# Layer 1's output projection as seven products of blocks, with weight sums made in DRAM, gate rows in the last head, and new orders from attention on

## The chip, the cores and the metric

The kernel runs on one core of a Trainium2 chip. The metric is the device time of one launch in microseconds. A core has a matrix engine (PE) with its weight loads (PEld), three engines for elementwise work (DVE, ACT and POOL), an engine SP that here only issues transfers, and DMA queues that carry data between DRAM and on-chip memory. Each engine works through its own instructions in program order and waits on semaphores for the others.

## The reference, cut to what matters

Two layers run over 512 latent and 256 context tokens of width 1024. Layer 0 is a hyena mixer and attention; layer 1, where the change lies, is a bidirectional mLSTM of eight heads with value width 256:

```python
def finish(h_f, h_b, o, z):
    h = (h_f + h_b).transpose(0, 2, 1, 3).reshape(Bn, n, ML_WIDTH).astype(o.dtype) * jax.nn.sigmoid(o)
    h = rms_norm(h.reshape(Bn, n, ML_HEADS, ML_V), head_norm.reshape(ML_HEADS, ML_V)).reshape(Bn, n, ML_WIDTH)
    return (h * jax.nn.silu(z)) @ w_out
...
x_lat = x_lat + ga_l[:, None] * rms_norm(y_lat, g_post[layer])
```

The product with w_out is 512 tokens x 2048 x 1024. Only the latent tokens are needed behind the last layer. ga_l is a third of silu(c) @ w_mod + b_mod: the "gate rows" below are these 1024 numbers, spread over all partitions and multiplied with g_post.

## The kernel before

All matrix products of activations with weights are made in three parts: each operand is split into a high part in a reduced float format (hi) and a remainder (lo), and `mm3` issues hi·hi, hi·lo and lo·hi into one PSUM tile. The ACT makes the high part by a cast, DVE the low part by a subtraction (`split`). `load_w` brings a block of weights in two chunks of 512 KB into raw tiles `wr` (three buffers) and splits them into one of two weight slots, `wh0/wl0` or `wh1/wl1`; the tiles then hold 8 k-tiles x 256 columns, or 4 k-tiles x 512 once they are viewed by `wide`.

The program is written as regions (start, hy, att, out0, l1a, l1b, out1). In each, the calls are recorded, and `play` issues them in the order of a table of numbers, ORDERS; a second table, SLOTS, says which buffer each tile takes. So all recorded instructions have one line in the profile, L1000 (L998 after the change), and are told apart by their tiles. Within an engine this order is program order.

Region l1b is the heads of layer 1. Each head has the state products, then a normalisation (tiles `num`, `dn`, `hh`, `hj`, `hst`, `hrs`), transposes through the PE into `pm`, and a store of the turned head, `y`, to `y1` in DRAM, 256 rows of 512 tokens. Between the products of a head `fill` places projections of the next head; the last head has the out gate (`out_gate`) and the gate z (`gate_z`) there, both with weights of the slots.

The output projection reads `y1` back. Its first 1024 rows of weights (heads 0 to 3) go as four stages of 256 columns, `pj` tiles of 128 tokens x 256: 4 stages x 4 token blocks x 8 k-tiles x 3 = 384 matmuls of 256 columns. The first stage's 96 are `ready` in region l1b, half of them ahead of the last head's transposes and half behind. The other 1024 rows go as 2 column halves x 2 parts x 4 blocks x 4 k-tiles x 3 = 192 matmuls of 512 columns, with the token tiles `hTh/hTl` and `ych/ycl`. All of it accumulates in `yacc`, half of it by DVE additions from PSUM.

In out1 `out_stages` calls `row(u)` and `spread(u)` of `gate_rows` between stages: `row` takes 2 MB of w_mod straight into a weight slot (two transfers of 1 MB) and runs 16 narrow matmuls for each of the halves hi and lo (`mod_rows`), `spread` turns the row into a tile with one wide matmul and multiplies it with g_post on DVE (`gg`). The end is `weigh1` (times gg), the squares of the ACT into `ss2`, `rstd` with a small POOL instruction (`ers`), and `epi1`, which scales, adds the residual `xt` and stores.

Earlier in the program, in region hy, the kernel already makes sums of weights in DRAM (`o_sums`) with copies that SP issues and accumulating transfers that POOL issues.

Of the kernel before, what the change touches and what calls it, by code (L numbers as in the profile page):

```python
# [2777 lines left out]
```

## Time and profile before

| what | us |
|---|---|
| three runs | 1490.02, 1491.35, 2872.85 |
| median | 1491.35 |
| profiled execution | 1491.61 |
| its span | 1489.8 |
| heads of layer 1 (l1b), from the span's start | about 1045 to 1392 |
| output projection of layer 1 behind the last head's transposes | 1392 to 1482 |

The profile comes from one execution of 1491.61 us. Its span, 1489.8 us, is the time between the first and the last recorded instruction. The highest of the three runs lies far from the other two, which agree within 0.1%. Busy times add up what an engine's instructions took; PE matmuls are pipelined and their ends are modelled, so that the mean of a single one in the groups is longer than the pace at which they follow one another. The pace is read from the chain of waits, where a row gives start, duration, engine and tile, and xN the number of instructions in the piece.

### The profile page before, as it was taken

The page shows a single profiled execution, that of the slowest core. Times are in us where ns is not written, and L with a number is a line of the kernel's source. Part 1 is how long each engine was busy: PE and PEld are TensorE (multiplying, and loading weights), DVE is VectorE, ACT ScalarE, POOL GpSimd, SP SyncE. Part 2 cuts the span into 40 slices and gives each one's busy share as a digit, 9 for nine tenths or more (in the row PEclk, how much of TensorE's full clock was granted, in tenths as well). Part 3 has the DMA queues.
Part 4 walks back from the last instruction along what each step waited for, and adds up shares of the span by engine and source line. Part 5 has one row for each costly group of instructions (what it writes and reads, how often), then busy time and mean ns, then how long its engine had stood idle before and what let it go on. Part 6 is the DMA issues. An engine that isn't in the chain of part 4 may idle for free. (4 is left out here: it accounts for less than half of the span.)

```text
span 1489.8 us, 25927 instructions
## 1 busy us (share of the span) xinstructions
PE 1457.7 (98%) x10362; PEld 1339.3 (90%) x10362; DVE 1037.1 (70%) x1927; ACT 766.3 (51%) x1577; POOL 82.5 (6%) x125
## 2 busy tenths in 40 slices
PE   7999999999999999999999989999999999999997
PEld 5889999989998998989997789999999999999986
DVE  6687777887865666668325888666777777877455
ACT  6634343434435444446332567645766676666442
POOL 1100000001010000000000100000100000100000
PEclk9999999999999999999999999999999999999999
DMA  9755565457331121233462334675433322324463
GB/s 378 221 140 144 146 162 131 147 140 183 76 100 43 54 96 54 82 117 114 164 222 68 134 123 155 203 267 198 156 117 97 113 62 86 124 88 140 153 205 123
DMA packets 57353, 205.79 MB, mean 138 GB/s; under 512 B 7003, under 2 KB 8539, under 8 KB 54448
## 3 DMA queue, kind: packets, MB, share of 16 engines
q1 hardware_dynamic: 50968, 181.85, 35.9%
q0 software_dynamic: 5392, 21.11, 7.4%
q8 instruction: 81, 1.33, 0.4%
q10 hardware_dynamic: 872, 1.18, 0.3%
q14 instruction: 40, 0.33, 0.1%
HBM read 182.06 MB, written 51.41 MB: 157 GB/s over the span
## 5 line engine op out<-in xcount | busy, mean ns | idle before, releaser
L1000 PE MATMUL pj<-wh,hTh 128*128 128x256 f32 (+2 forms) x1200 | 340.6, 290 | 0.8 <-ACT qjunk L1000 0.4
L1000 PE MATMUL pj<-wl,hTh 128*128 128x256 f32 (+2 forms) x1200 | 337.4, 287 | 0.3 <-DVE wl L1000 0.3
L1000 PE MATMUL pj<-wh,hTl 128*128 128x256 f32 (+2 forms) x1200 | 336.7, 288 | 0.0
L1000 PE MATMUL pj<-hTh,wh 128*128 128x512 f32 (+1 forms) x832 | 286.8, 346 | 0.4 <-DVE vl L1000 0.3
L1000 PE MATMUL pj<-hTl,wh 128*128 128x512 f32 (+1 forms) x832 | 285.4, 344 | 0.4 <-DVE hTl L1000 0.4
L1000 PE MATMUL pj<-hTh,wl 128*128 128x512 f32 (+1 forms) x832 | 285.5, 345 | 0.0
L1000 PEld LDWEIGHTS pj<-wh,hTh 128*128 128x128 f32 x1200 | 224.3, 189 | 6.2 <-issue 2.7
L1000 PEld LDWEIGHTS pj<-wl,hTh 128*128 128x128 f32 x1200 | 225.0, 189 | 2.9 <-DVE wl L1000 0.5
L1000 PEld LDWEIGHTS pj<-wh,hTl 128*128 128x128 f32 x1200 | 223.9, 189 | 3.5 <-issue 1.5
L1000 DVE TENSOR_TENSOR wl<-wr,wh 128x1024 fp32r<-128x1024 f32 (+1 forms) x142 | 171.4, 1213 | 63.9 <-ACT wh L1000 63.9
L1000 ACT CAST wh<-wr 128x1024 fp32r<-128x1024 f32 (+1 forms) x142 | 146.7, 1043 | 83.4 <-PE pj L1000 55.8
L1000 PEld LDWEIGHTS pj<-hTh,wh 128*128 128x128 f32 x832 | 156.6, 189 | 18.5 <-DVE vl L1000 1.1
L1000 PEld LDWEIGHTS pj<-hTl,wh 128*128 128x128 f32 x832 | 156.8, 189 | 17.9 <-DVE hTl L1000 0.7
L1000 PEld LDWEIGHTS pj<-hTh,wl 128*128 128x128 f32 x832 | 156.4, 188 | 18.0 <-DVE wl L1000 0.3
L1000 DVE TENSOR_TENSOR PTl<-pj,PTh 128x384 fp32r<-128x384 f32 (+1 forms) x80 | 41.1, 526 | 18.8 <-ACT PTh L1000 18.4
L1000 ACT CAST PTh<-pj 128x384 fp32r<-128x384 f32 (+1 forms) x80 | 35.6, 459 | 30.5 <-PE pj L1000 29.8
L1000 DVE TENSOR_TENSOR wl<-ch,wh 128x1024 fp32r<-128x1024 f32 x28 | 34.2, 1221 | 24.5 <-ACT wh L1000 24.4
L1000 DVE TENSOR_REDUCE mx<-s 128x1 f32<-128x768 f32 (+1 forms) x48 | 37.2, 775 | 11.4 <-PE s L1000 11.2
L1000 PE MATMUL pm<-Rh,dfa 128*128 128x256 f32 (+1 forms) x192 | 45.0, 305 | 0.0
L1000 DVE TENSOR_TENSOR med<-big 128x512 f32<-128x512 f32 (+1 forms) x48 | 40.4, 864 | 5.0 <-ACT big L1000 4.8
L1000 PE MATMUL s<-dfa,qTh 128*128 128x256 f32 (+1 forms) x160 | 42.8, 338 | 0.7 <-ACT hdh L1000 0.6
L1000 DVE SCALAR_TENSOR_TENSOR C<-C,apb,pj 128x258 f32<-128x258 f32 x64 | 30.8, 481 | 16.5 <-PE pj L1000 11.8
(374 smaller groups left out, 3172.1 us busy)
## 6 DMA issues: line engine op xcount, KB each, us to landing
wr<-in_e_w_in SPq DMA_DIRECT2D x52, 512.0 KB, 5.3
wr<-in_o_w_in SPq DMA_DIRECT2D x50, 512.0 KB, 5.2
o_sums<-in_o_w_in POOLq DMA_DIRECT2D x28, 512.0 KB, 7.1
ch<-o_sums SPq DMA_DIRECT2D x21, 512.0 KB, 4.9
wh<-in_w_mod SPq DMA_DIRECT2D x10, 1024.0 KB, 7.3
wl<-in_w_mod SPq DMA_DIRECT2D x9, 1024.0 KB, 7.6
wr<-in_e_w_out SPq DMA_DIRECT2D x16, 512.0 KB, 4.5
wr<-in_o_w_out SPq DMA_DIRECT2D x16, 512.0 KB, 4.6
```

Of the source, the lines that this page charges most:

```text
L1000: x = fn(*a, **k)
```

## The change

The projection becomes a product of two-by-two blocks with seven products in place of eight (the form of Strassen and Winograd). The tokens are cut into two blocks of 256 and the 2048 rows into heads 0 to 3 and 4 to 7, the columns into halves of 512, so that `w11, w12` come from the first thousand rows and `w21, w22` from the second. Each product is 256 tokens x 1024 x 512, 48 matmuls of 512 columns:

| product | tokens | weights | goes into |
|---|---|---|---|
| p1 | A11 | w11 | c11 and, as a base, c21 and c12 |
| q7 | D1 | t3 | c21 |
| q6 | F6 | t2 | c21, c12 |
| q3 | F3 | w22 | c12 |
| q5 | F5 | t1 | c22, c12 |
| p2 | A12 | w21 | c11 |
| q4 | A22 | t4 | c21 |

- The weight sums t1 to t4 stand in a new DRAM tensor `w_sums`. `out_sums` makes them in eight steps of four transfers of 512 KB each, issued behind heads 0 to 5 and 6; steps without a sum are copies of SP, the others accumulating transfers of POOL. The layout of the first half of w_out changes with it.
- The token forms are differences of blocks of y. In l1b POOL subtracts in place for D1; in out1 `forms(h)` loads heads h and 4 + h and POOL makes F6 and F5 (in place) and F3 (tile `yf3`), twelve subtractions of 128x512. Each form is then split by ACT and DVE: 20 splits of 128x512 in out1, where 8 stood before.
- p1 and q7 are in l1b, p1 with its first half ahead of the last transposes and its second behind. out1 has the other five.
- In out1 ten blocks of weights are loaded (20 chunks of 512 KB); with the 8 of p1 and q7 it is 28 for the projection, where 16 were. The three raw buffers and two slots stay.
- The gate rows move into the last head: `row(0)` between out_gate and gate_z, `spread(0)`, `row(1)` and `spread(1)` behind gate_z, into a tile `gg1` of a new pool.
- The tables of att, out0, l1a, l1b and out1 are new, and most of SLOTS. Those of start and hy are the same. l1b has 3871 entries instead of 3784, out1 426 instead of 661.

By engine the program has 9188 rows on the PE instead of 9391 (rows with xN count once), 1849 on DVE instead of 1821, 1376 on ACT instead of 1365, 129 on POOL instead of 102 and 375 on SP instead of 353.

The PE at the last head's transposes, before. The `pj` tiles here are the ready products (weights `wh_2470`, `wl_2471`, tokens `hTh`, `hTl`), the `pm` the transposes of `hh`:

```order
L1000 MATMUL pj_12064<-wh_2470_12056,hTl 128x256
L1000 MATMUL pj_12064<-wh_2470_12056,hTh 128x256
L1000 MATMUL pj_12066<-wh_2470_12056,hTh 128x256
L1000 MATMUL pj_12066<-wl_2471_12057,hTh 128x256
L1000 MATMUL pm_12055<-c_ident,hh_12041 128x128 x4
L1000 MATMUL pm_12054<-c_ident,hh_12041 128x128 x4
L1000 MATMUL pj_12067<-wh_2470_12056,hTh 128x256
L1000 MATMUL pj_12067<-wl_2471_12057,hTh 128x256
L1000 MATMUL pj_12067<-wh_2470_12056,hTl 128x256
```
The same place after. `pj_12078` and `pj_12079` are p1's two tiles, `pm_12052` the second gate row, `wh_2461` its weights, which lie in the slot that `wh_2485` takes next:

```order
L998 MATMUL pj_12079<-wl_2482_12071,hTh 128x512
L998 MATMUL pj_12079<-wh_2481_12070,hTl 128x512
L998 MATMUL pm_12069<-c_ident,hh_12055 128x128
L998 MATMUL pm_12068<-c_ident,hh_12055 128x128
L998 MATMUL pm_12052<-wh_2461_12050,cond_67 32x256 x5
L998 MATMUL pm_12069<-c_ident,hh_12055 128x128
L998 MATMUL pm_12068<-c_ident,hh_12055 128x128
L998 MATMUL pm_12069<-c_ident,hh_12055 128x128 x2
L998 MATMUL pm_12068<-c_ident,hh_12055 128x128
L998 MATMUL pm_12052<-wh_2461_12050,cond_67 32x256
L998 MATMUL pm_12068<-c_ident,hh_12055 128x128
L998 MATMUL pm_12052<-wh_2461_12050,cond_67 32x256 x2
```
Behind these come eight more of the row with `wl_2462`, and then p1 with the new slot:

```order
L998 MATMUL pm_12052<-wl_2462_12051,cond_67 32x256 x8
L998 MATMUL pj_12079<-wh_2485_12074,hTh 128x512
L998 MATMUL pj_12078<-wh_2485_12074,hTh 128x512
L998 MATMUL pj_12078<-wl_2486_12075,hTh 128x512
L998 MATMUL pj_12078<-wh_2485_12074,hTl 128x512
```
Before, the products around the transposes read one slot; now the row stands among the transposes, and the products behind it read the row's slot, newly filled.

DVE towards the end of out1, before: one weight split to a few additions and weightings of `yacc`.

```order
L1000 TENSOR_TENSOR yacc_2482_15884<-pj_15943,yacc_2482_15884 128x512
L1000 TENSOR_TENSOR yacc_2482_15884<-yacc_2482_15884,gg_15885 128x512
L1000 TENSOR_TENSOR yacc_2482_15884<-pj_15949,yacc_2482_15884 128x512
L1000 TENSOR_TENSOR yacc_2482_15884<-yacc_2482_15884,gg_15885 128x512
L1000 TENSOR_TENSOR yacc_2482_15884<-pj_15951,yacc_2482_15884 128x512
L1000 TENSOR_TENSOR wl_2552_15954<-wr_15955,wh_2551_15953 128x1024
L1000 TENSOR_TENSOR yacc_2482_15884<-yacc_2482_15884,gg_15885 128x512
L1000 TENSOR_TENSOR wl_2552_15954<-wr_15956,wh_2551_15953 128x1024
```
DVE towards the end of out1, after (`wl_2571` and `wl_2575` are q4's weights, `gg` the gate, `xt` the residual):

```order
L998 TENSOR_TENSOR wl_2571_16069<-wr_16071,wh_2570_16068 128x1024
L998 TENSOR_REDUCE ess_16079<-ss_2501_15999 128x1
L998 TENSOR_SCALAR esst_16080<-ess_16079 128x1
L998 TENSOR_TENSOR yacc_2502_16000<-yacc_2502_16000,gg_1586_11172 128x512
L998 TENSOR_REDUCE ess_16083<-ss_2501_15999 128x1
L998 TENSOR_SCALAR esst_16084<-ess_16083 128x1
L998 TENSOR_TENSOR yacc_2502_16000<-yacc_2502_16000,gg_1586_11172 128x512
L998 SCALAR_TENSOR_TENSOR xt_2578_16076<-yacc_2502_16000,ers_16081,xt_2578_16076 128x512
L998 TENSOR_TENSOR wl_2575_16073<-wr_16074,wh_2574_16072 128x1024
L998 SCALAR_TENSOR_TENSOR xt_2578_16076<-yacc_2503_16001,ers_16081,xt_2578_16076 128x512
L998 SCALAR_TENSOR_TENSOR xt_2578_16076<-yacc_2502_16000,ers_16085,xt_2578_16076 128x512
L998 TENSOR_TENSOR wl_2575_16073<-wr_16075,wh_2574_16072 128x1024
```
The epilogue of the first two token blocks now stands among the last weight splits.

POOL behind the last head's `hrs`, before: nothing but the four `ers`.

```order
L1000 TENSOR_TENSOR hrs_12052<-hst_12051,mhalf 128x4
L1000 TENSOR_TENSOR ers_15962<-esst_15961,mhalf 128x1
L1000 TENSOR_TENSOR ers_15967<-esst_15966,mhalf 128x1
L1000 TENSOR_TENSOR ers_15973<-esst_15972,mhalf 128x1
L1000 TENSOR_TENSOR ers_15979<-esst_15978,mhalf 128x1
```
After (`yraa` and `yrab` are the loaded heads h and 4 + h):

```order
L998 TENSOR_TENSOR yraa_16012<-yraa_16012,yrab_16013 128x2x256
L998 TENSOR_TENSOR yraa_16012<-yraa_16012 128x2x256
L998 TENSOR_TENSOR yf_2537_16035<-yrab_16013,yraa_16012 128x512
L998 TENSOR_TENSOR yraa_16014<-yraa_16014,yrab_16015 128x2x256
L998 TENSOR_TENSOR yraa_16014<-yraa_16014 128x2x256
L998 TENSOR_TENSOR yraa_16020<-yraa_16020,yrab_16021 128x2x256
L998 TENSOR_TENSOR yraa_16020<-yraa_16020 128x2x256
L998 TENSOR_TENSOR yf_2539_16037<-yrab_16021,yraa_16020 128x512
L998 TENSOR_TENSOR yf_2538_16036<-yrab_16015,yraa_16014 128x512
```
The subtractions of all four pairs stand there in a row, ahead of the `ers`; the two raw tiles of a pair rotate through two buffers each.

The diff, with its tables cut to a line:

```diff
@@ layout @@
-    o["o_w_out"] = slices(wo[:1024])
+    o["o_w_out"] = quarters(wo[:1024])
@@ ORDERS, SLOTS @@
     "att": [
...
@@ ahead of l1b @@
+    w11, w12 = (ins["o_w_out"][:, hf] for hf in range(2))
+    w21, w22 = (ins["o_w_out2"][:, hf] for hf in range(2))
+    wsum = nc.dram_tensor("w_sums", [4, 2, P, 8, 256], F32).ap()
+
+    def out_sums(step):
+        t = wsum
+        dst, src, add = ((t[0], w12, 0), (t[2], w12, 0), (t[0], w11, 1), (t[2], w22, 1),
+                         (t[1], t[0], 0), (t[1], w22, 1), (t[3], t[1], 0), (t[3], w21, 1))[step]
+        for q in range(2):
+            for k in range(2):
+                sl = slice(4 * k, 4 * k + 4)
+                if add:
+                    G.dma_start(dst[q, :, sl], src[q, :, sl], accum_op=ALU.add)
+                else:
+                    SP.dma_start(dst[q, :, sl], src[q, :, sl])
+
+    gg1 = T(es.enter_context(tc.tile_pool(name="gate", bufs=1, side="left", reuse_waits="tile")), "gg1", (P, 1, D))
@@ heads, last head @@
-            work = [(out_gate, i) for i in range(4)] + [(gate_z, i) for i in range(4)]
+            row, spread = gate_rows(gg1, gg1[:, 0], 1, 1)
+            work = [(out_gate, i) for i in range(4)] + [(row, 0)] + [(gate_z, i) for i in range(4)] + [(spread, 0), (row, 1), (spread, 1)]
@@ behind each head @@
+        for step in {6: (6, 7), 7: ()}.get(h, (h,)):
+            out_sums(step)
@@ end of l1b @@
+    def form(tiles, a):
+        return lambda k, j: tuple(x[:, k, a + j * P:a + (j + 1) * P] for x in tiles)
+
+    def part(ps, w, i, lhs, q):
+        for kt in range(4):
+            ins_ = mm3(ps, lhs(4 * q + kt, i), (w[0][:, kt], w[1][:, kt]), q == 0 and kt == 0, q == 1 and kt == 3)
+        return ins_
...
+        split(*[x[:, k:k + n, NL:NT] for x in hT_], raw[:, :, :256])
+        G.tensor_tensor(raw[:, :, 256:], raw[:, :, 256:], raw[:, :, :256], ALU.subtract)
...
+    ws = [wide(load_w(w11[q])) for q in range(2)]
+    p1 = [PJ() for _ in range(2)]
...
+    ws = [wide(load_w(wsum[2, q])) for q in range(2)]
+    q7 = [PJ() for _ in range(2)]
...
@@ out1 @@
+    def forms(h):
+        ra, rb = (T(op, f"yra{x}", (P, 2, NL), bufs=2) for x in "ab")
+        SP.dma_start(ra, y1[h])
+        SP.dma_start(rb, y1[4 + h])
+        kk = slice(2 * h, 2 * h + 2)
+        lo, hi = (slice(n * 256, (n + 1) * 256) for n in range(2))
+        G.tensor_tensor(ra[:, :, hi], ra[:, :, hi], rb[:, :, hi], ALU.subtract)
+        G.tensor_tensor(ra[:, :, lo], ra[:, :, lo], ra[:, :, hi], ALU.subtract)
+        split(*[x[:, kk] for x in f6], ra[:, :, lo])
...
+    w = load(t2, 0)
...
+    q6 = pair()
+    both(q6, F6, w, 0)
...
+    q4 = pair()
+    for j in range(2):
+        for q, x in enumerate((w, wn)):
+            part(q4[j], x, j, A22, q)
+        V.tensor_tensor(c21[:, j], q4[j], c21[:, j], ALU.subtract)
+        weigh(0, 2 + j)
+        epilogue(2 + j)
```

More of the change, by code (lines that the diff above doesn't have):

```diff
@@ L754 @@
     "pm@3": [
[4 rows of a table removed]
[4 rows of a table added]
     ],
     "g@4": [
-        0, 1, 0, 1, 0, 1, 0, 1,
+        1, 0, 1, 0, 1, 0, 1, 0,
     ],
     "x0s@4": [
-        0, 1, 0, 1, 0, 1, 0, 1,
+        1, 0, 1, 0, 1, 0, 1, 0,
     ],
@@ L853 @@
     "xn@9": [
-        1, 0, 1, 2, 2, 0, 1, 2, 0, 1, 0, 2,
+        0, 1, 0, 2, 2, 1, 0, 1, 1, 2, 0, 2,
     ],
@@ L885 @@
     ],
-    "yraw2@15": [
-        0, 1, 2, 3, 0, 1, 2, 3,
+    "yraa@15": [
+        0, 1, 0, 1,
+    ],
+    "yrab@15": [
+        0, 1, 0, 1,
+    ],
+    "yf3@15": [
+        1, 2, 3, 0,
     ],
     "ess@15": [
-        0, 0, 0, 0,
+        1, 1, 1, 1,
     ],
     "esst@15": [
-        0, 1, 0, 1,
+        1, 0, 1, 0,
     ],
@@ L896 @@
         0, 1, 0, 1,
-    ],
-    "xt@15": [
-        2, 0, 1, 3,
     ],
@@ L2719, in _body @@
     record("out1")
-    yacc = [T(op, f"yacc{hf}", (P, 4, 512)) for hf in range(1)]
-    gg = T(op, "gg", (P, 1, D))
-    yacc.append(T(op, "yacc1", (P, 4, 512)))
-    gp1 = T(op, "gp", (P, D))
     ss2 = T(op, "ss2", (P, 4, 2))
-    ych = T(op, "ych", (P, 4, NL), F32R)
-    ycl = T(op, "ycl", (P, 4, NL), F32R)
-    def load_y(k, dst):
-        raw = T(op, "yraw2", (P, NL), bufs=4)
-        SP.dma_start(raw, y1[k // 2, :, k % 2])
-        split(*dst, raw)
-    def load_b():
-        for k in range(8, 12):
-            load_y(k, y_tile(k))
@@ L2738, in load_c @@
-    def load_c():
-        for k in range(12, 16):
-            load_y(k, (ych[:, k - 12], ycl[:, k - 12]))
-    def weigh1(hf, i):
-        V.tensor_tensor(yacc[hf][:, i], yacc[hf][:, i], gg[:, 0, hf * 512:(hf + 1) * 512], ALU.mult)
-    def epi1(i, rs):
-        xt = T(op, "xt", (P, D), bufs=4)
+    c11, c12, c21, c22 = (T(op, f"yacc{n}", (P, 2, 512)) for n in range(4))
+    f6, b22 = ([T(op, f"{n}{x}", (P, KT, 256), F32R) for x in "hl"] for n in ("yf", "yb"))
+    for n in range(2):
+        T(op, f"xt{n}", (P, KT, 256))
@@ new lines, in _body, with second, third @@
+    F6, A22, A12, F5 = form(f6, 0), form(b22, 0), form(hT_, NL), form(hT_, 256)
+    def forms(h):
[7 more added lines that the diff above has]
+        split(*[x[:, kk] for x in f6], ra[:, :, lo])
+        def second():
+            x = T(op, "yf3", (P, 2, 256), bufs=4)
+            G.tensor_tensor(x, rb[:, :, lo], ra[:, :, lo], ALU.subtract)
+            split(*[t[:, kk] for t in f3], x)
+            split(*[x[:, kk, 256:512] for x in hT_], ra[:, :, hi])
+        def third():
+            split(*[x[:, kk, NL:NT] for x in hT_], rb[:, :, lo])
+            split(*[x[:, kk] for x in b22], rb[:, :, hi])
+        return second, third
@@ new lines, in load, with both, yt, weigh @@
+    def load(src, q):
+        return wide(load_w(src[q]))
+    def both(ps, lhs, w, q):
+        for j in range(2):
+            part(ps[j], w, j, lhs, q)
+    def yt(i):
+        return [x[:, i % 2] for x in ((c11, c12) if i < 2 else (c21, c22))]
+    def weigh(hf, i):
+        y = yt(i)[hf]
+        junk = T(op, "junk4", (P, 512), bufs=1)
+        S.activation(junk, y, AF.Square, accum_out=ss2[:, i, hf:hf + 1])
+        V.tensor_tensor(y, y, gg1[:, 0, hf * 512:(hf + 1) * 512], ALU.mult)
+    def epilogue(i):
+        ss = T(op, "ess", (P, 1), bufs=2)
+        V.tensor_reduce(ss, ss2[:, i], axis=AX.X, op=ALU.add)
+        tmp = T(op, "esst", (P, 1), bufs=2)
+        rs = T(op, "ers", (P, 1), bufs=2)
+        rstd(rs, ss, D, tmp)
+        xt = xts[i // 2][:, i % 2]
@@ L2749, in epi1, with pair @@
             sl = slice(hf * 512, (hf + 1) * 512)
-            V.scalar_tensor_tensor(xt[:, sl], yacc[hf][:, i], rs, xt[:, sl], ALU.mult, ALU.add)
+            V.scalar_tensor_tensor(xt[:, sl], yt(i)[hf], rs, xt[:, sl], ALU.mult, ALU.add)
             SP.dma_start(outs[0][0, i * P:(i + 1) * P, sl], xt[:, sl])
-    out_stages(op, ins["o_w_out"], ins["o_w_out2"],
-               Part(0, load_b, lambda kt, i: y_lhs(8 + kt, i)), Part(4, load_c, lambda kt, i: (ych[:, kt, i * P:(i + 1) * P], ycl[:, kt, i * P:(i + 1) * P])),
-               yacc, ss2, (0, 1, 2, 3), gate_rows(gg, gp1, 1, 1), weigh1, epi1, w=w_out, ready=ready, y_a=y_lhs, w1=w_out1)
+    def pair():
+        return [PJ() for _ in range(2)]
@@ new lines, in _body @@
+    t1, t2, t3, t4 = (wsum[n] for n in range(4))
+    fs = [forms(h) for h in range(3)]
+    for j in range(2):
+        S.copy(c11[:, j], p1[j])
+    w = load(t2, 0)
+    for j in range(2):
+        V.tensor_tensor(c21[:, j], q7[j], c11[:, j], ALU.subtract)
+    fs.append(forms(3))
+    wn = load(t2, 1)
+    q6 = pair()
+    both(q6, F6, w, 0)
+    w = load(w22, 0)
+    f3 = [T(op, f"xt{x}", (P, KT, 256), F32R) for x in range(2)]
+    F3 = form(f3, 0)
+    both(q6, F6, wn, 1)
+    for j in range(2):
+        V.tensor_tensor(c21[:, j], q6[j], c21[:, j], ALU.add)
+        V.tensor_tensor(c12[:, j], q6[j], c11[:, j], ALU.subtract)
@@ new lines, in _body @@
+    for a, _ in fs:
+        a()
+    wn = load(w22, 1)
+    q3 = pair()
+    both(q3, F3, w, 0)
+    w = load(t1, 0)
+    both(q3, F3, wn, 1)
+    for j in range(2):
+        V.tensor_tensor(c12[:, j], q3[j], c12[:, j], ALU.add)
+    for _, b in fs:
+        b()
+    wn = load(t1, 1)
+    q5 = pair()
+    both(q5, F5, w, 0)
+    w = load(w21, 0)
+    both(q5, F5, wn, 1)
+    for j in range(2):
+        V.tensor_tensor(c22[:, j], q5[j], c21[:, j], ALU.add)
+        V.tensor_tensor(c12[:, j], q5[j], c12[:, j], ALU.add)
@@ new lines, in _body @@
+    for j in range(2):
+        weigh(1, j)
+        weigh(1, 2 + j)
+    wn = load(w21, 1)
+    p2 = pair()
+    both(p2, A12, w, 0)
+    w = load(t4, 0)
+    both(p2, A12, wn, 1)
+    wn = load(t4, 1)
+    xts = [T(op, f"xt{x}", (P, 2, D)) for x in range(2)]
+    for j in range(2):
+        V.tensor_tensor(c11[:, j], p2[j], c11[:, j], ALU.add)
+    for j in range(2):
+        weigh(0, j)
+        epilogue(j)
+    q4 = pair()
+    for j in range(2):
+        for q, x in enumerate((w, wn)):
[3 more added lines that the diff above has]
+        epilogue(2 + j)
```

93 lines of the change are left out of this document (43 added, 50 removed), and 869 rows, old and new, of tables (ORDERS, SLOTS).

## The prediction

> **What bounds the kernel now.** I read the page first, then a table of stretches, then the chain that ended last, then the groups by line, each for the stretch of the last head and of the output projection.
>
> ```profile
> span 1489.8 us, 25927 instructions
> PE 1457.7 (98%) x10362; PEld 1339.3 (90%) x10362; DVE 1037.1 (70%) x1927; ACT 766.3 (51%) x1577; POOL 82.5 (6%) x125
> ```
> The PE is busy for 1457.7 of 1489.8 us, so a gain is PE work that goes, and a loss is a place where the PE newly waits. The stretches (PE, PEld, DVE, ACT and POOL busy, then clock, DMA share, GB/s) are layer 0's attention and output, layer 1's first stage, its middle heads, its last head, and the projection in two parts:
>
> ```profile
> 410.00:870.00 460.00, 450.68 (x3264) 409.42 (x3264) 286.24 (x626) 207.02 (x496) 24.98 (x27) 1.00 0.32 107
> 905.00:1045.00 140.00, 139.30 (x1162) 138.71 (x1160) 96.58 (x120) 82.94 (x113) 0.00 (x0) 1.00 0.64 215
> 1180.00:1350.00 170.00, 168.34 (x1234) 158.83 (x1233) 128.16 (x266) 112.17 (x279) 11.21 (x21) 1.00 0.33 107
> 1350.00:1391.80 41.80, 41.13 (x339) 40.30 (x338) 32.83 (x72) 28.71 (x72) 2.02 (x2) 1.00 0.18 55
> 1391.80:1425.50 33.70, 33.70 (x300) 30.23 (x299) 7.89 (x8) 11.70 (x22) 0.00 (x0) 1.00 0.71 247
> 1425.50:1481.80 56.30, 56.30 (x289) 47.23 (x287) 32.35 (x47) 18.53 (x34) 1.67 (x3) 1.00 0.45 157
> ```
> From 1391.8 to 1481.8 the PE never stops, at full clock, while DVE works 40.2 of 90.0 us. The chain (start, us, what) gives the pace and the ends:
>
> ```profile
> 1382.12 0.89 DVE num L1000 x2
> 1383.65 0.88 DVE hh L1000 x2
> 1388.51 1.02 POOL hrs L1000
> 1389.96 0.89 DVE hh L1000 x2
> 1390.89 1.16 PE pm L1000 x7
> 1392.05 11.04 PE pj L1000 x92
> 1403.09 1.00 PE pm L1000 x16
> 1405.72 1.00 PE pm L1000 x16
> 1410.52 0.86 PE pm L1000 x2
> 1425.55 56.30 PE pj L1000 x288
> 1481.87 0.70 DVE yacc L1000
> 1482.66 0.63 ACT junk L1000
> 1485.09 0.75 DVE xt L1000
> ```
> 92 products of 256 columns in 11.04 us are 0.120 us each. The last 288 are 96 of these and 192 of 512 columns, so one of 512 takes (56.30 − 96 × 0.120) / 192 = 0.2332 us. The first rows are the last head's normalisation, from the start of num to the first hh that the transposes (pm, x7) need: 1389.96 + 0.44 − 1382.12 = 8.3 us, wholly beside PE work, since the stretch up to 1391.8 has 0.67 us of PE idle in all. I call the end of these transposes T0.
>
> **PE work.** Before: 384 × 0.120 + 192 × 0.2332 = 46.1 + 44.8 = 90.9 us. After: 7 products × 48 = 336 × 0.2332 = 78.4 us. That is −12.5 us, certain as far as the PE stays dense. The gate rows' matmuls (two of 1.00 us for a row, 0.86 for a spread, twice) only change place.
>
> **The wait for the last head.** Behind the last state matmul the order of after has 24 products of 512 and one spread until the transposes: 24 × 0.2332 + 0.86 = 6.5 us beside a chain of 8.3 us, which the change leaves as it is. Before, gate and ready products covered it. I take +1.8 us; the bounds are 0 (work of other heads slips in) and 3 (the second row's weights come late). That row's weights, two transfers of 1 MB, can be asked for only when gate_z has read its slot, about where the chain begins:
>
> ```profile
> wr<-in_o_w_out SPq DMA_DIRECT2D x16, 512.0 KB, 4.6
> o_sums<-in_o_w_in POOLq DMA_DIRECT2D x28, 512.0 KB, 7.1
> wh<-in_w_mod SPq DMA_DIRECT2D x10, 1024.0 KB, 7.3
> ch<-o_sums SPq DMA_DIRECT2D x21, 512.0 KB, 4.9
> ```
> 7.3 us is inside 8.3 us, so they cost nothing by themselves, with 1 us to spare.
>
> **The wait behind the transposes.** Before, the second 48 ready products read the same weights as the first. Now p1's second half needs a weight slot that the second gate row holds until after the transposes, and the ACT does two y first. The costs, from the groups of 1391.8 to the end (mean ns behind the busy time):
>
> ```profile
> L1000 DVE TENSOR_TENSOR wl<-wr,wh 128x1024 fp32r<-128x1024 f32 x14 | 16.8, 1222 | 27.1 <-ACT wh L1000 27.1
> L1000 ACT CAST wh<-wr 128x1024 fp32r<-128x1024 f32 x13 | 13.4, 1049 | 12.7 <-PE pj L1000 6.4 <-DMA wr<-in_o_w_out 5.5 <-ACT mrow L1000 0.7
> L1000 DVE TENSOR_TENSOR yacc<-pj,yacc 128x512 f32<-128x512 f32 x12 | 8.3, 691 | 10.1 <-PE pj L1000 9.9
> L1000 DVE SCALAR_TENSOR_TENSOR xt<-yacc,ers,xt 128x512 f32<-128x512 f32 x8 | 5.6, 747 | 2.1 <-POOL ers L1000 2.1
> L1000 DVE TENSOR_TENSOR yacc<-yacc,gg 128x512 f32<-128x512 f32 x8 | 5.5, 690 | 5.0 <-ACT junk L1000 5.0
> L1000 DVE TENSOR_TENSOR ycl<-yraw,ych 128x512 fp32r<-128x512 f32 x4 | 2.8, 690 | 3.0 <-ACT ych L1000 3.0
> L1000 ACT CAST ych<-yraw 128x512 fp32r<-128x512 f32 x4 | 2.5, 622 | 1.4 <-DMA yraw<-y_scratch 1.4
> L1000 ACT ACTIVATE y<-pm,hnc 128x512 f32<-128x512 f32 x2 | 1.3, 686 | 3.0 <-PE pm L1000 3.0
> ```
> Two y (0.69 each), one cast (1.05) and one subtraction (1.22) are 3.65 us from T0. Against them stand ten of the row's sixteen matmuls (of 2.00 us, 1.25) and the two products hi·hi that need the cast alone (0.47). 3.65 − 1.25 − 0.47 = 1.9 us, and some 0.3 for the semaphores between: +2.2 us. Bounds: 0, should the planner's order find other work, and 3.65.
>
> **The stream of weights.** 28 half-megabyte chunks now instead of 16, each feeding 12 products, 2.8 us of PE instead of 5.6 to 5.8. The nearest row for that pace is the stretch from 905, where chunks of the same size feed 2.9 us of PE: 139.30 of 140.00 busy at 215 GB/s, with DVE at 96.58. There DVE does little else; here it does. From T0 to the last chunk's subtraction I count for DVE in the order of after: 26 weight splits × 1.222 = 31.8, 20 splits of token forms × 0.690 = 13.8, 14 PSUM adds × 0.691 = 9.7, 6 weightings × 0.690 = 4.1, 4 residuals × 0.747 = 3.0, 2 of the gate 1.4, small ones 0.6: 64.4 us. The PE needs 288 × 0.2332 + 2.1 of gate work = 69.3 us until then. So DVE goes from 45% to 93%, in program order, and a chunk is late whenever something stands ahead of it. The clear place is q4's second half: two residuals and a split stand ahead of its last split. I take 0.75 + 1.22 = +2.0 us; bounds 0 (93% is still below 100) and 5 (four such places, about one for each product in out1). ACT, with 1.05 a chunk and 0.62 a form, stays below DVE.
>
> **The subtractions on POOL.** Before, POOL does nothing for the projection but four small ers. Twelve subtractions of 128x512 are new in out1, and no row shows a POOL subtraction of that size. The nearest are selects of the same size (start, us, instruction), one beside a DVE that was about to start a short run, one beside two weight splits:
>
> ```profile
> 1215.91 0.64 POOL L1000 TENSOR_SCALAR_AFFINE_SELECT decay<-decay 128x512 f32<-128x512 f32 x1 [26.06 <-DMA decay<-nc_scratch]
> 1270.22 2.35 DVE L1000 TENSOR_TENSOR wl<-wr,wh 128x1024 fp32r<-128x1024 f32 x2
> 1270.36 2.70 POOL L1000 TENSOR_SCALAR_AFFINE_SELECT decay<-decay 128x512 f32<-128x512 f32 x1 [2.10 <-DMA decay<-nc_scratch]
> ```
> So a subtraction costs POOL between 0.64 and 2.70 us: the second select lasted until the two DVE splits of 2.35 us beside it had ended. The deadline is F6's last form, of heads 3 and 7, at about T0 + 32: 1.25 + 2.2 + 0.86, then 24 + 48 products (16.8), then q6's first half and half its second (8.4), and 2 us of slack for products that can go ahead. Its buffers come free after POOL's sixth subtraction, its load takes 4.9 (the ch row), and POOL's ninth and tenth, a cast and a split (1.3) follow. With the first pair landed at T0 + 9 (asked for when the last head's buffers are free, some 4 us behind T0, and 4.9 in flight; an estimate) that is T0 + 9 + 8 subtractions + 6.2: T0 + 20 at 0.64 each (the order on DVE then decides, near T0 + 30), T0 + 36.8 at 2.70. It passes the deadline from 2.1 us on. I take +0.5 us, near the lower end because DVE also runs adds with a PSUM operand between its splits; bounds 0 and 4.8. The Trainium skill ("SBUF — State Buffer", section "Who interferes with whom") says that a DVE instruction with two SBUF inputs and a GpSimd instruction that reads SBUF exclude each other for their whole length, whichever issues first; the pair at 1270 agrees, and by that rule the rival below takes the forecast's place. The skill's "GPSIMD Engine Reference", section "Elementwise — side-by-side cycle accounting", has an addition of two inputs on GpSimd at 1.96 times the DVE's time, an estimate of 1.35 us for one of these by the 0.69 above; with it this sum stays as it is, since 1.35 is below 2.1.
>
> **Covered parts.** The sums in DRAM are 16 copies on SP and 16 accumulating transfers on POOL, from 1045 to 1390. Issue costs POOL 0.82 us each:
>
> ```profile
> L1000 POOL DMA_DIRECT2D o_sums<-in_o_w_in x28 | 22.8, 816 | 334.1 <-DMA o_sums<-in_o_w_in 167.2 <-DMA o_sums<-o_sums 163.6 <-issue 3.2
> ```
> 28 of these stand in the kernel already, among heavier work. In the heads POOL is busy 11.21 of 170 us and the DMA share is 0.33, so I put them at 0; behind POOL's issue waits hrs, once a head, which the 8.3 us chain needs: bounds 0 and 8 × 0.82. The tail after the last product is two tiles' work on DVE instead of one: half a residual, +0.4 us, bounds 0 and 1.5.
>
> **Sum.** −12.5 + 1.8 + 2.2 + 2.0 + 0.5 + 0.4 = −5.6 us. The profiled execution took 1491.61 us, 1.8 more than its span and within 0.3 of the median, 1491.35; so 1491.6 − 5.6 = 1486.0.
>
> **Rivals.** (1) The PE stays dense: the planner's order finds cover for each wait. The stretch at 905 speaks for it, DVE's 93% against. 1491.6 − 12.5 = 1479.1. (2) POOL and DVE shut each other out, the case that ends above the time before. F6 is 4.8 us late instead of 0.5, and DVE loses 12 × 0.64 = 7.7 us: 64.4 + 7.7 = 72.1 against 69.3, 2.8 us more. 1486.0 + 4.3 + 2.8 = 1493.1; with two of q6's adds and a cast that then queue up (1.4 + 0.6), some 1495. It decides from a subtraction of 2.1 us on. The pair at 1270 speaks for it; against it, that DVE's two splits there took 1.18 each, no longer than alone. (3) The change does not do what it says where it counts: the new orders of attention, of layer 1's first stage and of the heads decide. There the PE idles 9.3 + 0.7 + 2.3 us in the stretches above, which is the most that they can win; they can lose as much. 1474 to 1500.
>
> **Numbers.** The forecast, 1482 to 1490 on its own, has 0.45; (1) 0.25; (2) 0.18; (3) 0.12, half on each side. A range from 1475 to 1496 leaves out most of (3) and the worse part of (2), 0.17 in all. A measurement here tells about 2% (30 us) from no change. Faster by that much needs, beyond the 12.5, over 17 of the 32.1 us that the PE idles in the span: 0.02, from (3). Slower by it: 0.04, from (3) and from (2) with every subtraction at 2.70 and DVE shut out as long (32.4 us).
>
> **What would show it.** In the profile of after: 336 products at 0.233 us; a PE wait of about 2 us ahead of the last transposes and one of about 2 behind them, released by DVE wl; DVE busy over 85% from T0 on, with q4 waiting for wl; POOL's subtractions below 2.1 us and no long wait for yfl. Wrong would be a PE without gaps (rival 1), subtractions of 2 us and more with q6 waiting (rival 2), or stretches before 1350 that differ by more than 5 us (rival 3).

## The result, and the profile after

The changed kernel takes 1500.24 us (median of 4 runs, 1498.73 to 1502.13) where the kernel before takes 1491.37: a ratio of 1.0065, 95% interval 1.0048 to 1.0082. It is slower by 0.65%, and above the predicted range (1475 to 1496). The profiled execution, the slowest of the four, took 1502.13 us with a span of 1500.4.

The head of the page of the changed kernel:

```profile
span 1500.4 us, 25608 instructions
PE 1454.9 (97%) x10122; PEld 1328.6 (89%) x10122; DVE 1073.5 (72%) x1955; ACT 779.8 (52%) x1587; POOL 121.1 (8%) x157
```

The PE is busy for 2.8 us less, not 12.5, in a span that is 10.6 us longer. PE busy counts a product at the clock that it got, so a slow clock shows as work. To see where the time went, both programs are cut at four places: the first product of layer 0's output projection that reads the tile yoh (about 780), the first of layer 1's first stage that reads f5h, the last transpose of the last head (T0), and the last product. In layer 0 the orders differ, so the first cut is not quite the same place: the changed kernel has done some 24 matmuls more by then (616 behind it up to the second cut, instead of 640). First the kernel before, then the changed one (PE, PEld, DVE, ACT, POOL busy, PE clock, DMA share, GB/s):

```profile
777.50:906.10 128.60, 121.77 (x640) 102.04 (x638) 95.23 (x174) 64.95 (x119) 8.94 (x15) 0.99 0.34 111
906.10:1391.80 485.70, 483.26 (x3705) 464.89 (x3706) 357.50 (x660) 318.16 (x692) 24.90 (x45) 1.00 0.42 136
1391.80:1481.80 90.00, 90.00 (x587) 77.45 (x585) 40.24 (x55) 30.23 (x55) 1.67 (x3) 1.00 0.55 190
```
```profile
782.20:913.50 131.30, 120.02 (x616) 100.39 (x615) 93.13 (x171) 62.99 (x116) 8.67 (x15) 0.96 0.30 103
913.50:1407.10 493.60, 488.52 (x3717) 466.22 (x3715) 363.18 (x662) 319.51 (x692) 42.18 (x65) 0.99 0.59 179
1407.10:1491.60 84.50, 78.66 (x336) 60.65 (x335) 68.94 (x78) 43.86 (x65) 22.27 (x14) 0.96 0.68 237
```

The stretch behind T0 is only 5.5 us shorter, although some 3.5 us of gate work have left it besides the products. The heads are 7.9 us longer, of which those 3.5 are moved work. Layer 1 starts 7.4 us late (913.5 instead of 906.1). All three stretches have a clock below that of before.

What the PE waited for in the changed kernel, from head 6 to the middle of out1 (us in total, times, longest):

```profile
PE pj L998 <- DVE wl L998: 5.5, 3, 4.7
PE pm L998 <- DVE hh L998: 3.3, 2, 2.3
```

Two long waits stand out, both on DVE: 2.3 us for hh of head 6, near 1362, and 4.7 us for the first weight split of t2, at 1427. The timeline shows DVE and POOL at the first of them (start, us, instruction):

```profile
1359.97 4.88 DVE L998 SCALAR_TENSOR_TENSOR hh<-hh,hrs,zs 128x256 f32<-128x256 f32 x3
```
```profile
1358.52 1.03 POOL L998 TENSOR_TENSOR hrs<-hst,mhalf 128x4 f32<-128x4 f32 x1 [15.13 <-DVE hst L998]
1359.55 2.21 POOL L998 TENSOR_TENSOR vl<-vl 128x768 f32<-128x768 f32 x1
1361.71 1.99 POOL L998 TENSOR_TENSOR vh<-vh 128x768 f32<-128x768 f32 x1
1363.67 0.90 POOL L998 TENSOR_TENSOR cvo<-cvo 128x256 f32<-128x256 f32 x1
```

Three hh instructions take 4.88 us here; two of the same kind took 0.89 us in the kernel before. Each lasts about as long as the POOL subtraction beside it (singly 2.07, 2.03 and 0.94 us; POOL's 2.21, 1.99 and 0.90). At the second wait the form splits do the same, DVE first, then POOL:

```profile
1425.33 1.79 DVE L998 TENSOR_TENSOR hTl<-yraa,hTh 128x512 fp32r<-128x512 f32 x1
1427.04 1.78 DVE L998 TENSOR_TENSOR hTl<-yrab,hTh 128x512 fp32r<-128x512 f32 x1
1428.74 1.75 DVE L998 TENSOR_TENSOR ybl<-yrab,ybh 128x512 fp32r<-128x512 f32 x1
1430.42 2.32 DVE L998 TENSOR_TENSOR wl<-wr,wh 128x1024 fp32r<-128x1024 f32 x1
1432.67 0.68 DVE L998 TENSOR_TENSOR yacc<-pj,yacc 128x512 f32<-128x512 f32 x1
```
```profile
1424.82 1.75 POOL L998 TENSOR_TENSOR yraa<-yraa,yrab 128x512 f32<-128x512 f32 x1
1426.64 1.63 POOL L998 TENSOR_TENSOR yraa<-yraa 128x512 f32<-128x512 f32 x1
1428.35 1.60 POOL L998 TENSOR_TENSOR yf<-yrab,yraa 128x512 f32<-128x512 f32 x1
```

A split of 0.69 us takes 1.75 to 1.79, a weight split of 1.22 takes 2.32; the addition that reads PSUM takes its usual 0.68. Behind the long waits of this execution, the two of layer 0 included, the PE runs at half its clock for a while:

```profile
846.40:849.80 3.40, 2.97 (x8) 2.40 (x9) 2.31 (x7) 1.60 (x3) 0.89 (x1) 0.50 0.00 0
873.70:880.50 6.80, 4.02 (x18) 3.75 (x18) 3.97 (x9) 3.27 (x7) 0.18 (x3) 0.50 0.79 275
1365.20:1372.00 6.80, 5.90 (x29) 5.79 (x28) 5.00 (x9) 3.95 (x11) 0.00 (x0) 0.50 0.23 77
1430.10:1436.90 6.80, 4.10 (x10) 3.27 (x11) 6.80 (x8) 0.91 (x2) 3.41 (x2) 0.50 0.58 171
```

These are 23.8 us at 0.50, with the PE busy for 17.0 of them: some 8.5 us of its time are lost. The kernel before has one such stretch of 3.4 us (from 867.6), all of it busy: 1.7 us. So 6.8 us more go to the slow clock, and the PE idles 13.4 us more (1500.4 − 1454.9 against 1489.8 − 1457.7). Less the 12.5 us of products that is 7.7 of the 10.6 us by which the span grew; the other 2.9 are not accounted for here.

### The profile page after: what moved, and what is told of

It is laid out like the page before. It is cut to its first block, busy times and chain, and to the rows that moved or that the text cites. A ratio compares the mean times of both kernels' runs of the same rounds, so it can differ in the third digit from the quotient of the medians.

```text
span 1500.4 us, 25608 instructions
## 1 busy us (share of the span) xinstructions
PE 1454.9 (97%) x10122; PEld 1328.6 (89%) x10122; DVE 1073.5 (72%) x1955; ACT 779.8 (52%) x1587; POOL 121.1 (8%) x157
## 5 line engine op out<-in xcount | busy, mean ns | idle before, releaser
L998 PE MATMUL pj<-wl,hTh 128*128 128x256 f32 (+2 forms) x1104 | 316.5, 292 | 1.9 <-DVE wl L998 1.9
L998 PE MATMUL pj<-wh,hTh 128*128 128x256 f32 (+2 forms) x1104 | 315.6, 293 | 0.9 <-ACT qjunk L998 0.5
L998 PE MATMUL pj<-wh,hTl 128*128 128x256 f32 (+2 forms) x1104 | 314.7, 292 | 0.0
L998 DVE TENSOR_TENSOR wl<-wr,wh 128x1024 fp32r<-128x1024 f32 (+1 forms) x154 | 188.7, 1231 | 50.7 <-ACT wh L998 50.5
L998 PEld LDWEIGHTS pj<-wh,hTh 128*128 128x128 f32 x1104 | 207.0, 189 | 7.9 <-issue 2.1
L998 PEld LDWEIGHTS pj<-wl,hTh 128*128 128x128 f32 x1104 | 208.1, 190 | 6.6 <-DVE wl L998 2.6
L998 PEld LDWEIGHTS pj<-wh,hTl 128*128 128x128 f32 x1104 | 206.7, 189 | 3.9 <-issue 0.5
L998 ACT CAST wh<-wr 128x1024 fp32r<-128x1024 f32 (+1 forms) x154 | 159.0, 1044 | 71.8 <-PE pj L998 39.0
L998 POOL DMA_DIRECT2D o_sums<-in_o_w_in x28 | 22.8, 814 | 334.5 <-DMA o_sums<-in_o_w_in 167.4
L998 ACT ACTIVATE qjunk<-pj 128x128 f32<-128x128 f32 x60 | 16.7, 278 | 55.3 <-PE pj L998 23.4
```

What stands on the lines that cost most here:

```text
L998: x = fn(*a, **k)
```

## The experiments

Three theories were tried: P, POOL's subtractions and DVE's instructions with two operands in SBUF hold each other up. O, the new orders up to layer 1's first stage cost time by themselves. D, against P: DVE has too much queued ahead of t2's split, whatever POOL does. Times are medians, each with the ratio to the kernel before and its interval.

**Subtractions cut to one column** (`tiny_subs`):

```diff
-            G.tensor_tensor(x, rb[:, :, lo], ra[:, :, lo], ALU.subtract)
+            G.memset(x, 0.0)
-        G.tensor_tensor(ra[:, :, hi], ra[:, :, hi], rb[:, :, hi], ALU.subtract)
+        G.tensor_tensor(ra[:, :, 256:257], ra[:, :, 256:257], rb[:, :, 256:257], ALU.subtract)
...
```

> The sixteen POOL subtractions of the token forms are cut to one column each (the third of a pair becomes a memset), so the forms are not those of the reference; every DVE, ACT, PE and DMA instruction stays. Theory P (POOL's subtractions and DVE's instructions with two SBUF inputs hold each other up): hh in head 6 falls from 2.07 us to 0.48, the form splits in out1 from 1.77 us to 0.69, the PE waits at 1362 (2.45 + 1.14 us) and 1427 (4.9 us) go, and with them the low clock behind them (2.6 and 2.3 us): 1500.2 - 6.2 - 7.2 = 1487. Theory D (DVE simply has too much queued ahead of t2's first split, POOL or not): the wait at 1427 stays above 3 us, and the time is 1493 or more.

1488.7 us, 0.9986 (0.9977 to 0.9996). Both waits and the slow clock behind them are gone, with the same DVE instructions:

```profile
912.00:1399.60 487.60, 485.89 (x3716) 463.84 (x3715) 359.89 (x662) 319.82 (x692) 37.14 (x65) 1.00 0.59 181
1399.60:1476.50 76.90, 76.08 (x336) 59.40 (x335) 59.22 (x79) 43.34 (x65) 6.69 (x14) 1.00 0.74 260
```

The heads are 6.0 us shorter than in the changed kernel, the stretch behind T0 7.6 us, and DVE is busy 59.22 us there instead of 68.94: POOL's twelve subtractions had cost DVE 9.7 us. (Both stretches together are 13.6 us shorter by these two profiled executions, but that of the changed kernel is its slowest; by the medians the run is 11.5 us faster.) The memsets that stand in four of their places cost DVE nothing that can be seen. The run takes away POOL's work and DVE's slowing together. That the slowing decides, and not that POOL's forms come late, is seen above, where DVE has next to no idle time ahead of t2's split and its instructions are longer, and from the small program below. D, that DVE is too full whatever POOL does, falls.

**D1's subtractions on DVE** (`l1b_subs_dve`):

```diff
-        G.tensor_tensor(raw[:, :, 256:], raw[:, :, 256:], raw[:, :, :256], ALU.subtract)
+        V.tensor_tensor(raw[:, :, 256:], raw[:, :, 256:], raw[:, :, :256], ALU.subtract)
```

> The four subtractions for D1 at the end of l1b move from POOL to DVE, the twelve of out1 stay. Theory P: hh in head 6 falls to 0.48 us and the PE waits ahead of and among its transposes (2.45 + 1.14 us, 2.6 more of low clock) go, less up to 1.5 us where the 2.7 us of new DVE work is in the way: 1494 to 1496. Theory D: DVE is as late as before, the waits stay, and the time is 1499 to 1502.

1496.2 us, 1.0035 (1.0022 to 1.0049): 4.1 us less than the changed kernel. The same three hh now take, from the timeline of DVE:

```profile
1360.37 1.27 DVE L998 SCALAR_TENSOR_TENSOR hh<-hh,hrs,zs 128x256 f32<-128x256 f32 x3
```

From there to the end of the heads the PE waits for hh once only, at the last head:

```profile
PE pm L998 <- DVE hh L998: 1.0, 1, 1.0
PE pj L998 <- DVE C L998: 0.5, 1, 0.5
```

So the whole wait at head 6 came from POOL beside DVE. DVE does the four subtractions itself at little loss: one new wait of 0.5 us.

**The new early orders in the kernel before** (`before_new_orders`) and **the old ones in the changed kernel** (`after_old_orders`). Both swap the same tables; the rest of each program stays:

```diff
-ORDERS["att"], ORDERS["out0"], ORDERS["l1a"]   of the one kernel, with their part of SLOTS
+ORDERS["att"], ORDERS["out0"], ORDERS["l1a"]   of the other kernel, with their part of SLOTS
```

> The kernel before with the new tables of att, out0 and l1a and their buffers; the heads and the projection are those of before. Theory O (the new order at the end of layer 0 costs by itself what the trace shows more of PE stall from 840 to 900, 4.8 us): 1491.4 + 4.5 = 1496, with the PE waiting 3.6, 2.8 and 3.1 us for xn transposes. Its rival, that this stall comes from traffic or state that only the whole change brings: 1490.5 to 1492.5.

> The changed kernel with the old tables of att, out0 and l1a and their buffers. Theory O: 1500.2 - 4.5 = 1495.7, with the PE's waits between 840 and 880 as in the kernel before (1.4 us at most). Its rival: 1499.5 to 1501.

1497.85 us, 1.0045 (1.0028 to 1.0061), is 7.2 us more than the kernel before; 1492.59 us, 1.0011 (1.0001 to 1.0020), is 7.7 us less than the changed kernel. O holds both ways, and the cost is larger than the 4.5 us that the waits alone had suggested. By the traces layer 1's first stage starts at 913.8 with the new orders and at 906.3 with the old ones, close to the changed kernel (913.5) and the kernel before (906.1). What the PE waited for between 838 and 880, first in the kernel before, then with the new orders:

```profile
PE pm L1000 <- DVE xn L1000: 3.7, 4, 1.0
PE pm L1000 <- DVE wa L1000: 1.3, 1, 1.3
```
```profile
PE pm L929 <- ACT hf L929: 3.4, 2, 2.9
PE pm L929 <- DVE hf L929: 3.4, 1, 3.4
```

Before, several waits of at most 1.3 us; now two near 3 us (2.9 and 3.4), at the transposes of the normalised tokens (`xn`, `hf`) behind layer 0's epilogue. From 840 to 880 the clock falls from 0.96 to 0.81 with them:

```profile
840.00:880.00 40.00, 34.13 (x198) 29.61 (x197) 34.05 (x71) 25.84 (x52) 5.48 (x11) 0.96 0.44 152
```
```profile
840.00:880.00 40.00, 30.10 (x138) 24.97 (x138) 29.66 (x66) 22.66 (x47) 5.36 (x10) 0.81 0.42 146
```

Between 844 and 882 that is 17.0 us at half clock, in three stretches, where the kernel before has its 3.4 us. Which of the moved instructions makes the two waits is not shown.

**Both at once** (`old_tiny`), the two edits above together:

> Both suspects at once: the old tables of att, out0 and l1a, and the sixteen POOL subtractions cut to one column each (so the forms are not those of the reference). If theories P and O are separate causes, their gains add: 1500.2 - 7.7 (old orders) - 11.5 (subtractions) = 1481, which is within 2 us of the dense PE (1491 - 12.5 = 1479), and the PE clock is full from 100 us to the last product. If they share a cause (the PE clock, or DMA traffic), they add less: 1485 or more.

1481.06 us, 0.9933 (0.9919 to 0.9948). The gains add, well within the noise: 1500.2 − 7.7 − 11.5 = 1481.0 (that it fits to the tenth is luck, as the interval is some 2 us to either side). They are two causes. No stretch of slow clock is left between the start of the program and the last product, and from head 6 on the PE waits only here:

```profile
PE pm L928 <- DVE hh L928: 1.0, 1, 1.0
PE pj L928 <- DVE wl L928: 0.5, 1, 0.5
PE pj L928 <- ACT wh L928: 0.3, 1, 0.3
```

**The subtractions of out1 on DVE** (`out1_subs_dve`), all twelve, in the table's old places:

```diff
-        G.tensor_tensor(ra[:, :, hi], ra[:, :, hi], rb[:, :, hi], ALU.subtract)
+        V.tensor_tensor(ra[:, :, hi], ra[:, :, hi], rb[:, :, hi], ALU.subtract)
...
```

> The twelve subtractions of out1 move from POOL to DVE, the four of l1b stay on POOL. Theory P: the form splits fall to 0.69 us, but DVE has 12 x 0.69 = 8.3 us more, some 3.5 of it ahead of t2's first split; the wait of 4.9 us at 1427 falls to about 2, and one window of low clock less: 1495 to 1498. Theory D (DVE's load alone decides): DVE has only more to do, the wait grows to 6 or more, 1502 and above.

1501.47 us, 1.0077 (1.0062 to 1.0092): no gain, a miss. The splits did fall to 0.69 us and the wait for t2 to 0.8, but in its place the PE waits for the forms:

```profile
PE pj L998 <- DVE yfl L998: 2.1, 1, 2.1
PE pj L998 <- DVE wl L998: 1.4, 2, 0.8
```

DVE now runs the subtractions in an order made for POOL, between splits that nothing needs yet.

**t2's split two places earlier** (`t2_first`), in the table of out1, where 22 is the weight split, 20 and 21 its load and cast, 185 and 187 the two form splits:

```diff
-101, 20, 8, 102, 185, 23, 187, 21, 18, 22,
+101, 8, 102, 20, 21, 22, 185, 23, 187, 18,
```

> Only the order of three instructions of out1 changes: DVE makes t2's first weight split two form splits earlier, everything stays on its engine. Theory P: each of these two splits takes 1.77 us beside POOL, so the wait at 1427 falls from 4.9 to 1.5 to 2 us, and with it one or both windows of low clock: 1494 to 1498. If the order is no part of it (the wait is the form's, which POOL makes late), the wait stays at 4 us or more: 1499 to 1501.

1500.93 us, 1.0064 (1.0047 to 1.0081): the same as without. Between 1400 and 1445 the PE still waits for weight splits, at the longest for t2's second one, which stands behind the same slow form splits:

```profile
PE pj L911 <- DVE wl L911: 5.9, 4, 3.5
```

With POOL beside it DVE's queue as a whole is late, and another place for one instruction did not mend it.

**The cost by itself** (`port_micro`): a program of its own, streams of 128x512 on POOL and DVE, and PE bursts with waits between.

> A program of its own that computes nothing of the reference. Part one: POOL subtractions of 128x512 alone, DVE subtractions of 128x512 alone, then both at once, POOL beside DVE with one operand in PSUM, POOL beside DVE with one input, and POOL memsets beside DVE subtractions. Theory P: alone POOL takes 0.9 to 1.4 us and DVE 0.69; both at once DVE's mean rises above 1.2 us and POOL's above 1.6; beside a PSUM operand and beside memsets both stay as alone. Against it: DVE stays at 0.69 in all parts. Part two: bursts of 72 PE products with waits between them of 1 to 6 ACT instructions (0.6 us each); the half clock of 3.4 or 6.8 us should follow waits from about 2.5 us on and not those below 1.5.

The timeline: eight POOL subtractions alone, DVE's alone, then both, then POOL beside a DVE with one operand in PSUM, and memsets beside DVE subtractions:

```profile
11.98 9.80 POOL L42 TENSOR_TENSOR gsub<-xa 128x512 f32<-128x512 f32 x8
26.34 9.12 DVE L48 TENSOR_TENSOR vsub<-xa 128x512 f32<-128x512 f32 x15 [1.15 <-POOL gsub L39]
40.20 22.45 DVE L48 TENSOR_TENSOR vsub<-xa 128x512 f32<-128x512 f32 x23 [1.15 <-POOL gsub L39]
40.24 13.44 POOL L42 TENSOR_TENSOR gsub<-xa 128x512 f32<-128x512 f32 x8
66.95 14.44 DVE L51 TENSOR_TENSOR vsub<-pv,xa 128x512 f32<-128x512 f32 x24 [1.37 <-POOL gsub L39]
67.00 9.85 POOL L42 TENSOR_TENSOR gsub<-xa 128x512 f32<-128x512 f32 x8
107.05 7.53 POOL L45 MEMSET gsub<- 128x512 f32 x16
```

Alone a POOL subtraction takes 9.80 / 8 = 1.23 us and one on DVE 9.12 / 15 = 0.61. Together POOL needs 13.44 / 8 = 1.68, and DVE does about one in each of these: (22.45 − 13.44) / 0.61 = 15 of its 23 come after POOL has ended, 8 beside it. In such rows they take turns. So a POOL subtraction costs DVE 1.68 − 0.61 = 1.07 us, more than the 0.61 of doing it itself. With an operand in PSUM neither is held up (14.44 / 24 = 0.60 and 9.85 / 8 = 1.23), and beside the memsets, which read nothing, DVE's 15 take 9.12 us as they do alone. The Trainium skill ("SBUF — State Buffer", section "Who interferes with whom") says that a DVE instruction with two SBUF inputs contends with a GpSimd instruction that reads SBUF, and not with one that only writes it. The rows at 40.2, 66.95 and 107.05 agree.

The second part, some of the PE bursts (in brackets the wait ahead of each):

```profile
158.72 16.61 PE L74 MATMUL pe<-hi,w 128*128 128x512 f32 x72 [1.35 <-ACT hi L79]
177.40 16.62 PE L74 MATMUL pe<-hi,w 128*128 128x512 f32 x72 [2.07 <-ACT hi L79]
196.69 18.22 PE L74 MATMUL pe<-hi,w 128*128 128x512 f32 x72 [2.67 <-ACT hi L79]
240.42 18.99 PE L74 MATMUL pe<-hi,w 128*128 128x512 f32 x72 [3.99 <-ACT hi L79]
398.98 18.24 PE L74 MATMUL pe<-hi,w 128*128 128x512 f32 x72 [2.07 <-ACT hi L79]
```

A burst of 16.61 us is 1.6 us longer behind a wait of 2.67, 2.4 us behind 3.99, and not longer behind 1.35. Of four waits of 2.07 us one was followed by a longer burst, the last row.

**Without the weight sums** (`no_sums`):

```diff
-                    G.dma_start(dst[q, :, sl], src[q, :, sl], accum_op=ALU.add)
+                    G.dma_start(dst[q, :1, sl], src[q, :1, sl], accum_op=ALU.add)
-    t1, t2, t3, t4 = (wsum[n] for n in range(4))
+    t1, t2, t3, t4 = w12, w11, w22, w21
...
```

> The 32 transfers of the weight sums move one partition instead of 128, and t1 to t4 are read from w_out itself, so the output is not the reference's; every instruction and every other transfer stays. If the sums are hidden, as the prediction had it: 1499 to 1501.5, with the same waits of the PE. If their 16 MB of copies and 16 MB of additions hold up loads, or POOL's issue holds up hrs: 1497 or less.

1500.41 us, 1.0061 (1.0046 to 1.0076): unchanged. The bytes of the sums are hidden. Their transfers are still issued in this run, so what the issue costs POOL is not tested by it; `old_tiny`, which has all of it, leaves some 1 us for it at most.

**Old early orders and D1 on DVE** (`old_l1b`), two of the edits above together:

> The old tables of att, out0 and l1a, and D1's four subtractions on DVE; out1 as in the changed kernel. By adding what the two runs gave apart: 1500.2 - 7.7 - 4.1 = 1488.4, below the kernel before (1490.5); the PE's wait of 4 to 5 us at t2's first split stays. If the two share a part of their gain: 1490 or more.

1488.34 us, 0.9981 (0.9972 to 0.9990), as the two runs apart had given.

**out1 ordered for DVE** (`best_v`), and **the same on POOL** (`best_g`). On top of `old_l1b`, the forms that q6 reads are made first, five splits for the later products (ten instructions of ACT and DVE) move behind them, and the raw tiles get more buffers; `best_v` has the twelve subtractions on DVE, `best_g` on POOL:

```diff
-        ra, rb = (T(op, f"yra{x}", (P, 2, NL), bufs=2) for x in "ab")
+        ra, rb = (T(op, f"yra{x}", (P, 2, NL), bufs=n) for x, n in (("a", 3), ("b", 4)))
-        G.tensor_tensor(ra[:, :, hi], ra[:, :, hi], rb[:, :, hi], ALU.subtract)
+        V.tensor_tensor(ra[:, :, hi], ra[:, :, hi], rb[:, :, hi], ALU.subtract)
...
```

> old_l1b, and in out1 all twelve subtractions on DVE, with the forms that q6 needs made first, the splits for q5, p2 and q4 later, and three and four raw buffers instead of two and two, so that the last pairs are loaded early. Theory P (a POOL subtraction costs DVE about 1.0 us beside it, one on DVE 0.61) with DVE's order freed: PE waits of 1 to 3 us in q6 instead of 7.6 in all, 1482 to 1485. If DVE's load binds whatever the order: 1488 to 1491.

> best_v with the twelve subtractions on POOL. Theory P: the same order, but each of DVE's splits beside a subtraction takes 1.65 us; slower than best_v by 1 to 4 us, with POOL's chain of ten subtractions of 1.65 us (16.5 us) the end of F6. If POOL takes work off DVE after all: faster than best_v.

best_v takes 1484.06 us, 0.9954 (0.9939 to 0.9969), and is faster than both kernels, by half a per cent than the one before. best_g takes 1491.32 us, 1.0004 (0.9994 to 1.0014): the same order is 7.3 us slower with the subtractions on POOL, more than the 1 to 4 expected. It is also 3.0 us slower than `old_l1b`, which has POOL's subtractions in the old order. So neither half of the step gains by itself: DVE in POOL's order (`out1_subs_dve`) gained nothing, POOL in DVE's order lost, and only the two together win. The stretch behind T0 in best_v:

```profile
1393.10:1473.20 80.10, 77.02 (x336) 59.01 (x335) 66.30 (x89) 43.44 (x65) 1.79 (x2) 1.00 0.70 250
```

DVE works 66.30 us of 80.1. That is 7.1 us more than in `tiny_subs`, its twelve subtractions at 0.6 each, and less than the 68.94 of the changed kernel, where POOL made them. What is left there against `tiny_subs` (76.9) are 3.2 us; 2.0 of them are longer waits for weight splits.

## Why the prediction was wrong, step by step

| step | predicted | shown by | measured |
|---|---|---|---|
| products, 384 + 192 to 336 | −12.5 | old_tiny: 1490.3 − 12.5 + 1.0 + 0.8 + 0.7 = 1480.3 against 1481.06 | −12.5 fits within 1 us (by these medians; not measured apart) |
| wait for the last head | +1.8 | wait of the PE, `hh` (old_tiny) | +1.0 |
| wait behind the transposes | +2.2 | `wl` 0.5, `wh` 0.3 (old_tiny) | +0.8 |
| DVE's 93%, q4 late | +2.0 | no wait in q4 in any run | 0 |
| POOL's subtractions | +0.5 | tiny_subs, slow clock included | +11.5 |
| sums in DRAM | 0 | no_sums (the bytes alone) | 0 |
| tail | +0.4 | last product to the end, 8.0 to 8.7 (old_tiny) or 8.8 | +0.7 |
| orders of att, out0, l1a | 0 | both swaps, slow clock included | +7.2 to +7.7 |

- **POOL's subtractions** are the step that failed. The prediction put them at +0.5 us, "near the lower end". It looked for the cost at the last form of F6, as POOL's own lateness. It came elsewhere: POOL's subtractions slowed the DVE instructions beside them, and these made t2's split and head 6's hh late. The row that it held against this rival, two DVE splits at 1270 "no longer than alone", shows only a single POOL instruction that waited for a DVE already running: in a row of POOL instructions the two take turns, and then DVE pays. The four subtractions of l1b were not in the sum at all; 4.1 us of the 11.5 are theirs. Rival (2) had this mechanism and put 0.64 us a piece on DVE's queue, with a chance of 0.18. The small program gives 1.07 us, and the rival, too, counted neither l1b nor the slow clock.
- **The early orders** are the second step that failed: the sum has nothing for them. They were a rival with 0.12, half of it for a loss, and with a bound from the PE's idle time. That bound limits what an order can win, not what it can lose; as it stands (12.3 us) it would give 1498.3 at most, not 1500. The loss was found in two longer waits and the slow clock behind them; why the new order has these waits stays open.
- **The rivals were kept apart.** They name different places of the program, so their prices add: rival (2), some 9 us above the forecast at 1495, and the 7 us that the orders came to give 1502. The range had room for one such loss and not for both.
- **The slow clock** was missing from every term. A long wait is paid once as a wait and mostly again as half clock: in the small program 1.5 to 2.4 us behind waits of 2.67 to 3.99, at most half of 3.4 or 6.8.
- **DVE's load** was overstated: the count took recorded durations, 0.69 and 1.22 us, while instructions follow one another after 0.61 and 1.14. In `tiny_subs` they take 59.2 us behind T0 instead of the 64.4 that were summed, 77% of 76.9 us, and the PE waits nowhere in q4, in any run.

Right were the products' price, that the sums in DRAM are hidden, and the two waits around the last head by place, at half the size. Less than 2% either way was said at 0.94.

## What to carry to other kernels

Before an elementwise instruction with two SBUF operands is moved to POOL, look at what DVE does at that moment: beside DVE's own two-operand instructions it costs DVE more time (1.07 us for 128x512) than doing it there (0.61). Moving it back helped at once in l1b, and in out1 only with an order made for it. A wait of the matrix engine is to be priced with the slow clock that may follow it, which was the rule behind waits of 3 us here and the exception behind waits of 1. Where several things may go wrong in different places of a program, their prices are added in the range, and a new order of work that "should do the same" is measured by itself.
